# VectorE gating, a 64x64 triangular inverse and a loop set inside the sum, in a hybrid attention, RWKV-7 and expert block

## The chip, the cores and the metric

The kernel runs on one core of one Trainium2 chip. The metric is device time in microseconds (us) of one execution of the whole block. The engines are TensorE (PE for matmuls, PEld for its weight loads), VectorE (DVE), ScalarE (ACT), GpSimd (POOL) and SyncE (SP, which issues DMAs here).

## What is computed

One decoder layer over 256 tokens of width 2048: eight heads of attention beside sixteen heads of RWKV-7 time mixing, an output projection, then a mixture of 128 x 128 single-neuron experts, of which each token takes 16 in each of 8 heads. What matters of the reference:

```python
def rwkv7_time_mix(...):                       # 16 heads of 64
    def step(state, inp):
        rt, wt, kt, vt, at, bt = inp
        sa = jnp.einsum('bhij,bhj->bhi', state, at)
        state = (state * wt[:, :, None, :] + sa[..., None] * bt[:, :, None, :]
                 + vt[..., :, None] * kt[..., None, :])
        y = jnp.einsum('bhij,bhj->bhi', state, rt)
        return state, y

def peer_ffn(x, wq, sub_keys, u, v):
    q = (xt @ wq).reshape(T, H, 2, PEER_HALF)
    s = jnp.einsum('thpc,hpnc->thpn', q, sub_keys).astype(jnp.float32)
    sv, si = lax.top_k(s, K)
    cand = (sv[:, :, 0, :, None] + sv[:, :, 1, None, :]).reshape(T, H, K * K)
    best, bi = lax.top_k(cand, K)
...
    expert = (i1 * PEER_NKEYS + i2).astype(jnp.int32)
    gates = jax.nn.softmax(best, axis=-1)
    def chunk(args):
        xc, ec, gc = args
        hpre = jnp.einsum('cd,chkd->chk', xc, u[ec]).astype(jnp.float32)
        act = (jax.nn.gelu(hpre, approximate=False) * gc).astype(x.dtype)
        return jnp.einsum('chk,chkd->cd', act, v[ec])

def reference(...):
        h = h + jnp.concatenate([attn, rw], axis=-1) @ w_out[l]
        h = h + peer_ffn(rmsnorm(h, norm2_g[l]), peer_wq[l], peer_sub_keys[l], peer_u[l], peer_v[l])
    return rmsnorm(h, final_g)
```

## The kernel before, in words

All matmuls are made nearly float32 by splitting an operand into a high and a low part, each multiplied in one pass. For weights, `prefetch` loads a half of a weight block ("raw", 512 KB, SP), ScalarE rounds it to the high part (`whi`, L204) and VectorE subtracts to get the low part (`wlo`, L205). Three slots hold split halves, so that about two halves are ready ahead of PE. The list `halves` gives the order in which all weights are loaded and split. The order of the instructions on each engine is set by a scheduler at build time: generators `yield` numbers that say how much time a piece of work is meant to take, and the scheduler puts pieces side by side by those; nothing is reordered at run time, and each engine works strictly in its order.

The stages, by what PE does. *Projections* (7 to 540 us): `products()` runs the loras, then eight head pairs of RWKV (three blocks of weights each, L218 to L220), then eight attention heads; after each piece, `step_all` moves up to four live chains (`rwkv`, `attn`) on by a step. An `rwkv` chain treats two heads of 64 at once, as a block diagonal 128x128 matrix in each of four chunks. It has to invert a unit triangular matrix, and does so in five doublings (L484 to L505): VectorE transposes X (L493), PE multiplies M by it (L496, `pw`), VectorE masks the product into `wm` (L498), PE multiplies that by XT (L502, `px`), VectorE adds to XT (L504). That is 5 doublings x 8 pairs = 40 groups on each of the two matmul lines. *Output* and *queries* follow (540 to 736), with scores and choices of experts prepared.

*Hidden stage* (736 to 1568): for each of the 128 keys (a key is 128 experts), 16 matmuls on L240 and 16 on L242 give the experts' first products; the low parts' sum is `part` (L1137 on ScalarE, L1138 on VectorE), and ScalarE applies gelu (L1122) into `A`, eight keys to a tile. Beside this run, paced by the list `beside`, the choices of experts (`both_choices`), the tables of gates (`tables`, written to memory as `gate_d`), `places`, which gives every expert a row in a list sorted by which of the two token tiles chose it, and `scatter`: as soon as places are known, near 1219, for each key the gates (`gt`, loaded by GpSimd for eight keys at a time from `gate_d`, L1075) are multiplied on `A` (L1093, on GpSimd but for the last two keys), and GpSimd sends the gated rows to their places with an indirect DMA (L1107).

*Sum* (1573 to 2029): the sorted rows are read back in blocks of 128 experts (L1200, SP), each block's second weights are gathered by an indirect DMA (L1205, GpSimd), both are split (L248 ScalarE, L249 VectorE), and PE adds the products into eight accumulators, four for each token tile (L1192 to L1194, 12 matmuls a tile and block). There are C0 = 28 blocks for tile 0 alone, C1 = 28 for tile 1 alone and MID = 52 for both, 24 matmuls each. Experts chosen by both tiles beyond 52 blocks would be summed by a run-time loop (L1264) whose count is read from `nblk`; it stands behind all unrolled blocks, and its body closes the accumulators. Behind it VectorE adds the accumulators to the residual (`yr`, L1295), and the last norm and the stores follow.

Of the kernel before, what the change touches and what calls it, by code (L numbers as in the profile page):

```python
# [10 lines left out]
F32 = mybir.dt.float32  # L11
F32R = mybir.dt.float32r
BF16 = mybir.dt.bfloat16
I32 = mybir.dt.int32
# [48 lines left out]
C0, C1, MID, DN = 28, 28, 52, 2  # L63
# [5 lines left out]
def consts():  # L69
# [6 lines left out]
    c[:, K_MSK:K_MSK + P] = same & (p[:, None] < p[None])  # L76
# [3 lines left out]
    for i in range(6):  # L80
        n = 1 << i
        lv = (p[:, None] // (2 * n) == p[None] // (2 * n)) & (p[:, None] % (2 * n) >= n) & (p[None] % (2 * n) < n)
        c[:, K_LV + i * P:K_LV + (i + 1) * P] = lv
        if i == 0:
            c[:, K_M1T:K_M1T + P] = lv.T
# [69 lines left out]
def block_kernel(ctx: ExitStack, tc: tile.TileContext, x, cols, consts, w_lora, w_gate, w_rkv, w_qkv,  # L155
# [25 lines left out]
    for w, n in ((w_gate, 2), (w_rkv, 3 * RJ), (w_qkv, 3 * AH)):  # L181
        halves += [(w[m, i].rearrange("p k c -> p (k c)"), HK * P) for m in range(n) for i in range(2)]
# [163 lines left out]
    wms = [p1.tile([P, NC, P], F32, name=f"wm{i}") for i in range(1, 6)]  # L346
# [8 lines left out]
    mska = kc(K_MSK, 128).rearrange("p (h t) -> p h t", h=2).unsqueeze(1).to_broadcast([P, 2, 2, CH])  # L355
    mskr = kc(K_MSK + 128, 192).unsqueeze(1).to_broadcast([P, 2, 192])
# [3 lines left out]
    idb = ident.unsqueeze(1).to_broadcast([P, NC, 128])  # L360
# [15 lines left out]
    def rwkv(j, r, k, vv):  # L376
# [82 lines left out]
        for q in range(0, NC, 2):  # L459
            pc = bank("pc", [P, 4, 128])  # L460
            for c in range(2):
                for i, src in enumerate((nbd, kbd)):
# [3 lines left out]
            nc.vector.tensor_tensor(M[:, q:q + 2, 0:128].rearrange("p a (h t) -> p a h t", h=2),  # L466
                                    pc2[:, :, 0:CH].unsqueeze(2).to_broadcast([P, 2, 2, CH]), mska, op=ALU.mult)
            nc.vector.tensor_tensor(M[:, q:q + 2, 128:320], pc2[:, :, CH:], mskr, op=ALU.mult)
            yield

        XT = W("XT", [P, NC, 128], 2)
        lv = lambda i: kc(K_LV + i * 128, 128)
        nc.vector.tensor_tensor(XT, M[:, :, 0:128], kc(K_M1T, 128).unsqueeze(1).to_broadcast([P, NC, 128]),
# [10 lines left out]
        for i in range(1, 6):  # L484
            n = 1 << i
            nblk = P // (2 * n)
# [13 lines left out]
            px = bank("px", [P, NC, CH])  # L500
            for c in range(NC):
                nc.tensor.matmul(o4(px)[:, c], wm[:, c, :], hi_(XT)[:, c], start=(c == 0), stop=(c == NC - 1),  # L502
                                 skip_group_check=True)
            nc.vector.tensor_tensor(hi_(XT), hi_(XT), o4(px), op=ALU.add)  # L504
            yield  # L505

        y = tmp("y", "y")[:, :S]
        Z = None
        for c in range(NC):
# [15 lines left out]
            nc.tensor.matmul(sa_p, XT[:, c, :], r0, start=True, stop=True)  # L525
# [113 lines left out]
    def products():  # L639
# [18 lines left out]
        for j in range(RJ):  # L658
            while len(live) > 4:
                step_all()  # L660
# [12 lines left out]
        state["pools"] = [spl]  # L673
        for h in range(AH):
            while len(live) > 4:
                step_all()
# [8 lines left out]
            clear(1)  # L685

# [236 lines left out]
    def table(t):  # L923


        while t not in chosen:
            yield 0
# [77 lines left out]
    def places():  # L1005
# [39 lines left out]
        for t, n, base in ((0, C0, 0), (1, C1, B1)):  # L1045
# [5 lines left out]
            yield 1.5  # L1051
# [28 lines left out]
    def gated(i2, eng=nc.gpsimd):  # L1080

        if i2 % 7 == 0:
            rows[0] = big("at")
            n = min(7, NKEY - i2)
            eng.tensor_copy(rows[0][:, 0:n * ROW].rearrange("p (n c) -> p n c", c=ROW)[:, :, T].bitcast(I32),
                                  eint[:, i2:i2 + n])
# [6 lines left out]
        eng.tensor_tensor(at[:, 0:T].rearrange("p (q t) -> p q t", q=KT),  # L1093
# [4 lines left out]
    def scatter():  # L1098
# [4 lines left out]
        for i2 in range(NKEY - DN):  # L1103
# [11 lines left out]
            yield 1.5  # L1115
# [38 lines left out]
    beside = [[both_choices(), 0.55, 0.0], [tables(), 0.38, 0.0], [scatter(), 1.0, 0.0]]  # L1154
# [168 lines left out]
```

## Time and profile before

| | us |
|---|---|
| median of 3 runs | 2051.95 (2043.92 to 2052.5) |
| profiled execution | 2048.21 |
| its span, first to last instruction | 2046.3 |
| PE busy | 1935.7 (95%) |
| VectorE busy | 1437.7 (70%) |
| ScalarE busy | 1062.9 (52%) |
| GpSimd busy | 712.1 (35%) |

The span is what the trace covers; the 1.9 us between it and the execution's time lie around it. Busy time of PE counts overlapping records from the first start to the last modelled end, so that 95% does not mean that PE does 95% of what it could: how far apart the same matmuls start tells more. The mean granted clock was 0.981 of full speed. The rows below are from this one execution; times in them are us from the span's start.

### The profile page before, as it was taken

Reading aid. Unit: us, or ns where it says so; the run is one execution under the profiler, and the core shown is the slowest. Engines: PE = TensorE matmul, PEld = TensorE weight load, DVE = VectorE, ACT = ScalarE, POOL = GpSimd, SP = SyncE. Lnnn points to the kernel's source line nnn. Section 1 sums busy time; section 2 is a strip of 40 time slices with the busy share of each in tenths; the row PEclk is TensorE's granted clock in tenths of the full one; section 3 lists DMA queues with packets and bytes.
Section 4 is the critical chain, followed back from the end, with each engine's and each line's share of the span. In section 5 each row is a group of like instructions: output and inputs, shape, how many; then the busy total and the mean of one; then the engine's idle time right before and its main releaser. Section 6 shows DMA issues by size and latency. Waiting matters only on the chain. (4 is left out here: it accounts for less than half of the span.)

```text
span 2046.3 us, 31447 instructions
## 1 busy us (share of the span) xinstructions
PE 1935.7 (95%) x11804; PEld 1723.3 (84%) x11804; DVE 1437.7 (70%) x2090; ACT 1062.9 (52%) x1696; POOL 712.1 (35%) x654
## 2 busy tenths in 40 slices
PE   7888999999999999999999999887998999999996
PEld 6788999999879998878888888776887788888885
DVE  6766878766556888999878866544755666666665
ACT  4534554345455444677676744433444555555554
POOL 7211211100000000023424269998986333333322
PEclk9999999999999999999999999998999999999998
DMA  8999322225576666556666678786888887878783
GB/s 248 258 247 246 98 87 87 88 83 146 190 227 198 184 180 188 173 175 197 215 195 217 196 237 264 248 267 229 270 267 271 343 284 280 296 286 293 281 297 141
DMA packets 135291, 443.91 MB, mean 217 GB/s; under 512 B 14369, under 2 KB 52257, under 8 KB 118497
## 3 DMA queue, kind: packets, MB, share of 16 engines
q1 hardware_dynamic: 106992, 289.24, 47.7%
q0 software_dynamic: 28144, 152.65, 20.4%
q8 instruction: 93, 1.52, 0.3%
q14 instruction: 62, 0.50, 0.1%
HBM read 380.07 MB, written 61.76 MB: 216 GB/s over the span
## 5 line engine op out<-in xcount | busy, mean ns | idle before, releaser
L205 DVE TENSOR_TENSOR wlo<-raw,whi 128x1024 fp32r<-128x1024 f32 (+1 forms) x408 | 569.6, 1402 | 301.1 <-ACT whi L204 291.9
L240 PE MATMUL ps_gm<-nx,whi 128*128 128x512 f32 x2048 | 731.8, 400 | 24.9 <-ACT whi L204 21.9
L204 ACT ACTIVATE whi<-raw 128x1024 fp32r<-128x1024 f32 (+1 forms) x408 | 429.5, 1055 | 384.2 <-issue 89.5
L242 PE MATMUL ps_gm<-nx,wlo 128*128 128x256 f32 x2048 | 579.4, 283 | 14.2 <-DVE wlo L205 14.2
L240 PEld LDWEIGHTS ps_gm<-nx,whi 128*128 128x128 f32 x2048 | 387.8, 189 | 112.6 <-ACT whi L204 22.6
L242 PEld LDWEIGHTS ps_gm<-nx,wlo 128*128 128x128 f32 x2048 | 390.3, 191 | 20.1 <-DVE wlo L205 19.7
L249 DVE TENSOR_TENSOR vlo<-vraw,vhi 128x2048 fp32r<-128x2048 f32 x108 | 247.9, 2297 | 151.6 <-ACT vhi L248 146.1
L248 ACT ACTIVATE vhi<-vraw 128x2048 fp32r<-128x2048 f32 x108 | 205.9, 1913 | 156.3 <-DVE vlo L249 146.8
L1205 POOL DMA_INDIRECT vraw<-in_v_dram,ag x108 | 145.1, 1343 | 294.8 <-PE ps_gm L1194 210.0
L218 PE MATMUL ps_gm<-xh,whi 128*128 128x256 f32 x640 | 192.7, 301 | 0.8 <-ACT whi L204 0.8
L220 PE MATMUL ps_gm<-xh,wlo 128*128 128x256 f32 x640 | 185.1, 289 | 3.2 <-DVE wlo L205 3.1
L219 PE MATMUL ps_gm<-xl,whi 128*128 128x256 f32 x640 | 185.6, 290 | 0.0
L1107 POOL DMA_INDIRECT rows_d<-at,place x126 | 169.5, 1345 | 36.9 <-POOL at L1093 15.8
L951 POOL TENSOR_TENSOR mt<-gc 128x1024 f32<-128x1024 f32 x16 | 39.7, 2482 | 345.5 <-ACT gc L979 345.5
L1122 ACT ACTIVATE A<-part 128x256 f32<-128x256 f32 x128 | 53.1, 415 | 166.7 <-DVE part L1138 131.3
L1093 POOL TENSOR_TENSOR at<-A,gt 128x256 f32<-128x256 f32 x126 | 129.2, 1041 | 5.4 <-DMA gt<-gate_d 3.6
L220 PEld LDWEIGHTS ps_gm<-xh,wlo 128*128 128x128 f32 x640 | 122.8, 192 | 4.6 <-DVE wlo L205 4.2
L218 PEld LDWEIGHTS ps_gm<-xh,whi 128*128 128x128 f32 x640 | 122.9, 192 | 1.9 <-ACT whi L204 1.2
L219 PEld LDWEIGHTS ps_gm<-xl,whi 128*128 128x128 f32 x640 | 122.9, 192 | 0.7
L807 POOL DMA_DIRECT2D skb<-in_sk_dram x16 | 8.6, 540 | 250.7 <-ACT mh L248 167.7
L945 ACT ACTIVATE ob<-ob,pick 128x128 f32<-128x128 f32 x256 | 83.9, 390 | 19.6 <-DVE ob L937 19.6
L373 POOL TENSOR_TENSOR df<-ext 128x256 f32<-128x256 f32 (+1 forms) x28 | 23.8, 850 | 155.3 <-DVE ext L371 142.4
(1521 smaller groups left out, 3925.5 us busy)
## 6 DMA issues: line engine op xcount, KB each, us to landing
raw<-in_u_dram SPq DMA_DIRECT2D x256, 512.0 KB, 4.1
raw<-in_w_rkv_dram SPq DMA_DIRECT2D x48, 512.0 KB, 7.3
raw<-in_w_qkv_dram SPq DMA_DIRECT2D x48, 512.0 KB, 3.6
rows_d<-zt SPq DMA_DIRECT2D x23, 1028.0 KB, 15.8
raw<-in_w_out_dram SPq DMA_DIRECT2D x32, 512.0 KB, 3.9
raw<-in_wq_dram SPq DMA_DIRECT2D x32, 512.0 KB, 3.6
gate_d<-gc SPq DMA_DIRECT2D x16, 1024.0 KB, 6.5
gt<-gate_d POOLq DMA_DIRECT2D x16, 1024.0 KB, 9.0
```

The costliest lines, as they stand in the source:

```text
L204: nc.scalar.activation(hi[:, :n], raw[:, :n], AF.Copy)
L205: state["dve"] = nc.vector.tensor_tensor(lo[:, :n], raw[:, :n], hi[:, :n].bitcast(F32), op=ALU.subtract)
L218: nc.tensor.matmul(ps, a, xh(kt), start=first and k == 0, stop=False)
L219: nc.tensor.matmul(ps, a, xl(kt), start=False, stop=False)
L220: state["mm"] = nc.tensor.matmul(ps, b, xh(kt), start=False, stop=last and k == HK - 1)
L240: nc.tensor.matmul(ps.rearrange("p z t -> p (z t)"), hi[:, k * P:(k + 1) * P], x_.rearrange("p z t -> p (z t)"), start=i + k == 0, stop=Fa ...
L242: state["mm"] = nc.tensor.matmul(ps[:, 0, :], lo[:, k * P:(k + 1) * P], x_[:, 0, :], start=False, stop=i == 1 and k == HK - 1, skip_group_ ...
L248: nc.scalar.activation(hi, src, AF.Copy)
L249: nc.vector.tensor_tensor(lo, src, hi.bitcast(F32), op=ALU.subtract)
L1093: eng.tensor_tensor(at[:, 0:T].rearrange("p (q t) -> p q t", q=KT), As[i2 // 8][:, k, :].rearrange("p (q t) -> p q t", q=KT), g.rearrange( ...
L1107: s_ = nc.gpsimd.indirect_dma_start(out=rows_d, out_offset=bass.IndirectOffsetOnAxis(ap=place[:, i2:i2 + 1], axis=0), in_=at, in_offset=None)
L1205: nc.gpsimd.indirect_dma_start(out=raw, out_offset=None, in_=vf, in_offset=bass.IndirectOffsetOnAxis(ap=ag[:, T:ROW].bitcast(I32), axis=0))
```

## The change

The diff, cut to its core:

```diff
-C0, C1, MID, DN = 28, 28, 52, 2
+C0, C1, MID, DN = 28, 28, 51, 2
...
+    ORDER = [("r", 0), ("r", 1)] + [x for j in range(2, RJ) for x in (("r", j), ("a", j - 2))] + [("a", AH - 2), ("a", AH - 1)]
...
-    wms = [p1.tile([P, NC, P], F32, name=f"wm{i}") for i in range(1, 6)]
+    wms = [p1.tile([P, NC, CH], F32, name=f"wm{i}") for i in range(1, 6)]
...
+    both = [slice(0, 64), slice(64, 128)]
...
-        XT = W("XT", [P, NC, 128], 2)
+        XT = W("XT", [P, NC, CH], 2)
...
-            X = W("X", [P, NC, 128], XB)
+            X = W("X", [P, NC, CH], XB)
             nc.vector.transpose(X.rearrange("p c s -> p (c s)"), XT.rearrange("p c s -> p (c s)"))
-            pw = bank("pw", [P, NC, CH])
+
+            pw = bank("pw", [P, NC, CH // 2])
             for c in range(NC):
-                nc.tensor.matmul(o4(pw)[:, c], M[:, c, 0:128], lo_(X)[:, c], start=(c == 0), stop=(c == NC - 1),
-                                 skip_group_check=True)
+                for hs in both:
+                    nc.tensor.matmul(o4(pw)[hs, c], M[hs, c, 64:128], lo_(X)[hs, c], start=True, stop=True,
+                                     skip_group_check=True)
...
+        XB_ = W("XB", [P, NC, 128], 2)
+        bd(XB_, XT)
...
+        for k, (what, n) in enumerate(ORDER):
+            while len(live) > 4:
+                step_all()
+            if what == "a":
+                state["pools"] = [spl]
+            yield from (pair if what == "r" else head)(n)
...
-        while t not in chosen:
+        while 0 not in chosen or 1 not in chosen:
...
-            yield 1.5
+            yield 2.6
...
-    def gated(i2, eng=nc.gpsimd):
+    def gated(i2):
...
-        eng.tensor_tensor(at[:, 0:T].rearrange("p (q t) -> p q t", q=KT),
+        nc.vector.tensor_tensor(at[:, 0:T].rearrange("p (q t) -> p q t", q=KT),
...
-            yield 1.5
+            yield 2.0
...
-    beside = [[both_choices(), 0.55, 0.0], [tables(), 0.38, 0.0], [scatter(), 1.0, 0.0]]
+    beside = [[both_choices(), 0.6, 0.0], [tables(), 0.45, 0.0], [scatter(), 1.0, 0.0]]
...
+        if k == 40:
+
+            count = nc.values_load(nblk[0:1, 0:1], min_val=0, max_val=128,
+                                   skip_runtime_bounds_check_because="a count of at most 16384 experts in blocks of 128")
+            with tc.For_i(MID, count, 1) as i:
+                rows[2] = rows[1]
+                ag, _ = rows_at(i * P + BM)
+                rows[1] = rows[2]
+                block((0, 1), *divided(ag, gather(ag)), False)
```

Four things, then. VectorE makes all multiplies by the gates and the small copies of row numbers beside them; GpSimd keeps the loads of `gt` and the scatters, and the numbers that pace `scatter`, `places`, `both_choices` and `tables` are others (the tables of both tiles start when both choices are done). The triangular inverse keeps each head's 64x64 matrix by itself: the two heads of a pair lie on partitions 0 to 63 and 64 to 127, masks, X, XT and `wm` are 64 columns wide instead of 128, each doubling has eight matmuls of 64x64 weights by 32 columns where it had four of 128x128 by 64, and one block diagonal (`XB`) is made at the end, by GpSimd, for the steps that follow. The projections' blocks come interleaved, RWKV pairs 0, 1, 2, attention head 0, pair 3, head 1 and so on, and the list of halves with them. And 51 blocks for both tiles are unrolled instead of 52, with the run-time loop set inside the unrolled sequence; the last unrolled block of each tile closes its accumulators.

Line numbers of the changed kernel are a little higher: L1093 becomes L1106, L1107 L1120, L1075 L1088, L205 L211, L1138 L1151, L496 L502, L502 L509, L1264 L1278.

GpSimd, from the first gates on, before: each multiply of `A` by `gt` stands ahead of the scatter (`rows_d`) of its row, and the loads of the next `gt` between them.

```order
L1075 DMA gt_13032<-gate_d 128x16x128
L1085 COPY at<-eint 128x7
L1075 DMA gt_13060<-gate_d 128x16x128
L1093 TENSOR_TENSOR at<-A_8199,gt_13032 128x256 x7
L1107 DMA rows_d<-at,place 39936x257 x7
L1085 COPY at<-eint 128x7
L1093 TENSOR_TENSOR at<-A_8199,gt_13032 128x256
L1093 TENSOR_TENSOR at<-A_8687,gt_13060 128x256
L1107 DMA rows_d<-at,place 39936x257 x2
L1075 DMA gt_13178<-gate_d 128x16x128
L1093 TENSOR_TENSOR at<-A_8687,gt_13060 128x256 x2
```

The same place on GpSimd after:

```order
L1088 DMA gt_13443<-gate_d 128x16x128
L1088 DMA gt_13476<-gate_d 128x16x128
L1120 DMA rows_d<-at,place 39936x257 x9
L1088 DMA gt_13624<-gate_d 128x16x128
L1120 DMA rows_d<-at,place 39936x257 x8
L1088 DMA gt_13783<-gate_d 128x16x128
L1120 DMA rows_d<-at,place 39936x257 x4
L1088 DMA gt_13937<-gate_d 128x16x128
L1120 DMA rows_d<-at,place 39936x257 x12
```

The multiplies are gone from GpSimd; a load of `gt` stands behind 4 to 14 scatters. They are now on VectorE, after `place` is written (L1073), among the low parts of the weights (L211) and the sums `part` (L1151), of which there is one a key:

```order
L1073 CAST place<-wk 128x128
L1098 COPY at<-eint 128x7
L211 TENSOR_TENSOR wlo<-raw,whi 128x1024
L1151 TENSOR_TENSOR part<-part,ps_gm 128x256
L1106 TENSOR_TENSOR at<-A_8539,gt_13443 128x256 x5
L211 TENSOR_TENSOR wlo<-raw,whi 128x1024
L1106 TENSOR_TENSOR at<-A_8539,gt_13443 128x256 x3
L1106 TENSOR_TENSOR at<-A_9039,gt_13476 128x256
L211 TENSOR_TENSOR wlo<-raw,whi 128x1024
L1151 TENSOR_TENSOR part<-part,ps_gm 128x256
L1106 TENSOR_TENSOR at<-A_9039,gt_13476 128x256 x5
```

Before, VectorE had only L205 and L1138 there. Between this `part` and the next two stand nine multiplies and then seven; further on come keys with none.

PE at the loop, after: the loop's count and branch stand behind the products of the first 36 blocks, and matmuls of the unrolled blocks follow behind the loop's body.

```order
L1207 MATMUL ps_gm<-vhi,al__17545 128x512
L1276 TENSOR_LOAD nblk
L1278 COMPARE_AND_BRANCH
L1278 UNCONDITIONAL_BRANCH x2
L1334 BRANCH_PREFETCH_HINT
L1205 MATMUL ps_mm<-vhi,ah 128x512
```

Before, the same rows stood behind the products of the last block:

```order
L1194 MATMUL ps_gm<-vhi,al__19260 128x512
L1262 TENSOR_LOAD nblk
L1264 COMPARE_AND_BRANCH
L1264 UNCONDITIONAL_BRANCH x2
L1318 BRANCH_PREFETCH_HINT
L1192 MATMUL ps_mm<-vhi,ah 128x512
```

The loop moved forward past 71 blocks on PE, and on the other engines past the blocks that they had prepared.

## Rows read from the trace of the kernel before

**Rows 1.** Table of windows, by stage; x is the number of instructions
```profile
core 0: us, PE busy (x) PEld busy (x) DVE busy (x) ACT busy (x) POOL busy (x), PEclk, DMA share, GB/s
0.00:200.00 200.00, 164.67 (x1251) 157.84 (x1252) 134.59 (x220) 86.95 (x137) 68.42 (x107) 0.97 1.01 252
200.00:540.00 340.00, 335.06 (x2695) 325.22 (x2694) 249.42 (x494) 159.40 (x301) 37.26 (x46) 1.00 0.35 104
840.00:960.00 120.00, 111.79 (x680) 98.20 (x679) 119.38 (x182) 81.79 (x169) 29.21 (x18) 1.00 0.58 181
1219.00:1568.00 349.00, 318.11 (x1774) 274.55 (x1773) 201.68 (x167) 148.75 (x222) 310.95 (x276) 0.96 0.79 256
1568.00:1592.00 24.00, 14.70 (x51) 11.09 (x49) 8.47 (x10) 9.24 (x13) 6.90 (x7) 0.80 0.96 341
1600.00:2000.00 400.00, 400.00 (x1766) 331.22 (x1765) 257.92 (x197) 219.38 (x196) 131.09 (x98) 1.00 0.81 290
...
1375.00:1400.00 25.00, 7.82 (x29) 6.38 (x30) 4.92 (x5) 5.27 (x8) 22.41 (x25) 0.59 0.48 155
```

**Rows 2.** The table of windows for line L240 alone (PE, PEld, PEclk, DMA)
```profile
740.00:840.00 100.00, 100.00 (x289) 53.87 (x289) 1.00 0.65 189
1219.00:1568.00 349.00, 314.68 (x887) 168.55 (x886) 0.96 0.79 256
```

**Rows 3.** Waits of ScalarE, 1219 to 1568: total us, times, longest us
```profile
ACT A L1122 <- POOL at L1093: 30.7, 2, 21.8
```

**Rows 4.** Groups of VectorE (busy us, mean ns), 740:840, then 1219:1568
```profile
L205 DVE TENSOR_TENSOR wlo<-raw,whi 128x1024 fp32r<-128x1024 f32 x36 | 43.7, 1215 | 11.4 <-ACT whi L204 11.3
...
L205 DVE TENSOR_TENSOR wlo<-raw,whi 128x1024 fp32r<-128x1024 f32 x110 | 182.7, 1675 | 146.8 <-ACT whi L204 138.9 <-PE ps_gm L240 6.0 <-PE ps_gm L242 1.4
L1138 DVE TENSOR_TENSOR part<-part,ps_gm 128x256 f32<-128x256 f32 x55 | 22.6, 410 | 0.0
```

**Rows 5.** Instructions of L1093: ns min/median/max, first and last start
```profile
L1093 POOL TENSOR_TENSOR at<-A,gt x126: 843/942/1997, 1205.2 to 1562.2; 128x256 f32<-128x256 f32 x126
L1093 DVE TENSOR_TENSOR at<-A,gt x2: 621/662/704, 1567.1 to 1572.9; 128x256 f32<-128x256 f32 x2
```

**Rows 6.** The page's groups: the scatter (busy us, mean ns, idle before)
```profile
L1107 POOL DMA_INDIRECT rows_d<-at,place x126 | 169.5, 1345 | 36.9 <-POOL at L1093 15.8
```

**Rows 7.** Line L1075, the loads of gt: from issue to landing
```profile
DMA to landing us min/median/max: 6.6/9.0/9.9
```

**Rows 8.** Instructions of line L496: ns min/median/max
```profile
L496 PEld LDWEIGHTS ps_pw<-X,M x320: 186/192/192, 96.7 to 431.3; 128*128 128x128 f32 x160
L496 PE MATMUL ps_pw<-X,M x320: 217/275/295, 96.8 to 431.4; 128*128 128x64 f32 x160
```

**Rows 9.** Timeline of PE (start, us): a group and the next matmul
```profile
246.70 1.00 PE L496 MATMUL ps_pw<-X,M 128*128 128x64 f32 x8
247.52 0.36 PE L218 MATMUL ps_gm<-xh,ml 128*128 128x256 f32 x1
```

**Rows 10.** Groups by form: a weight load of 96 columns
```profile
L220 PEld LDWEIGHTS ps_px<-xh,wlo 128*96 128x96 f32 x8 | 1.3, 162 | 0.0
```

**Rows 11.** Instructions of L493 (transpose) and L498 (multiply)
```profile
L493 DVE STREAM_TRANSPOSE X<-XT x40: 685/702/714, 95.6 to 429.8; 128x512 f32<-128x512 f32 x40
...
L498 DVE TENSOR_TENSOR wm<-ps_pw,kr x40: 356/425/427, 97.9 to 432.3; 128x256 f32<-128x256 f32 x40
```

**Rows 12.** The timeline at the end: last matmul, first and last addition
```profile
2028.80 0.39 PE L1194 MATMUL ps_gm<-vhi,al__19260 128*128 128x512 f32 x1
2029.58 0.69 DVE L1295 TENSOR_TENSOR yr<-yr,ps_mm 128x512 f32<-128x512 f32 x1 [7.86 <-PEq L1264]
...
2037.63 0.67 DVE L1295 TENSOR_TENSOR yr<-yr,ps_gm 128x512 f32<-128x512 f32 x1
```

**Rows 13.** The loop's line, PE's sequencer
```profile
L1264 PEldq EVENT_SEMAPHORE  x13: 51/51/51, 2029.2 to 2031.0; - x13
```

**Rows 14.** Line L1205, the gathers: from issue to landing
```profile
DMA to landing us min/median/max: 5.3/7.2/17.0
```

More of the change, by code (lines that the diff above doesn't have):

```diff
@@ L75, in consts @@
     same = p[:, None] // 64 == p[None] // 64
-    c[:, K_MSK:K_MSK + P] = same & (p[:, None] < p[None])
+    c[:, K_MSK + 64:K_MSK + P] = (p[:, None] % 64) < np.arange(64)[None]
     c[:, K_MSK + P:K_MSK + 192] = (p[:, None] % 64) <= np.arange(64)[None]
@@ L180, in block_kernel @@
         halves += [(w_lora[m, i].rearrange("p k c -> p (k c)"), HK * LOR) for m in range(2)]
-    for w, n in ((w_gate, 2), (w_rkv, 3 * RJ), (w_qkv, 3 * AH)):
-        halves += [(w[m, i].rearrange("p k c -> p (k c)"), HK * P) for m in range(n) for i in range(2)]
+    ORDER = [("r", 0), ("r", 1)] + [x for j in range(2, RJ) for x in (("r", j), ("a", j - 2))] + [("a", AH - 2), ("a", AH - 1)]
+    blocks_ = [(w_gate, m) for m in range(2)]
+    for what, n in ORDER:
+        blocks_ += [((w_rkv if what == "r" else w_qkv), 3 * n + i) for i in range(3)]
+    halves += [(w[m, i].rearrange("p k c -> p (k c)"), HK * P) for w, m in blocks_ for i in range(2)]
     KP = (4, 5, 6, 7, 0, 1, 2, 3)
@@ L490, in rwkv @@
             wm = wms[i - 1]
[L492 removed]
+            X = W("X", [P, NC, CH], XB)
             nc.vector.transpose(X.rearrange("p c s -> p (c s)"), XT.rearrange("p c s -> p (c s)"))
[L494 removed]
+            pw = bank("pw", [P, NC, CH // 2])
             for c in range(NC):
[L496 to L497 removed]
+                for hs in both:
+                    nc.tensor.matmul(o4(pw)[hs, c], M[hs, c, 64:128], lo_(X)[hs, c], start=True, stop=True,
+                                     skip_group_check=True)
             nc.vector.tensor_tensor(lo_(wm), o4(pw), lo_(lv(i).unsqueeze(1)).to_broadcast([P, NC, nblk, n]), op=ALU.mult)
             yield
[L500 removed]
+            px = bank("px", [P, NC, CH // 2])
             for c in range(NC):
[L502 to L503 removed]
+                for hs in both:
+                    nc.tensor.matmul(o4(px)[hs, c], wm[hs, c, :], hi_(XT)[hs, c], start=True, stop=True,
+                                     skip_group_check=True)
             nc.vector.tensor_tensor(hi_(XT), hi_(XT), o4(px), op=ALU.add)
             yield
+        XB_ = W("XB", [P, NC, 128], 2)
+        bd(XB_, XT)
         y = tmp("y", "y")[:, :S]
@@ L524, in rwkv @@
             sa_p = bank("ch", [P, 128])
-            nc.tensor.matmul(sa_p, XT[:, c, :], r0, start=True, stop=True)
+            nc.tensor.matmul(sa_p, XB_[:, c, :], r0, start=True, stop=True)
             sa = W("sa", [P, 128], 3)
@@ L657, in products, with pair @@
         state["pools"] = [spl, spl, spare[0]]
-        for j in range(RJ):
-            while len(live) > 4:
-                step_all()
+        def pair(j):
             got = []
@@ L672, in products, with head @@
             clear(2)
[L673 to L676, printed above, removed]
+        def head(h):
             got = []
@@ L1223, in block_kernel @@
         with tc.issue_after(state["gelu"].ins), tc.issue_after(u_end.ins):
-            ah, al_ = halves_of(gated(i2, nc.vector)[:, 0:T])
+            ah, al_ = halves_of(gated(i2)[:, 0:T])
         for i in range(2):
@@ L1260, in block_kernel @@
                 block((t,), *cut[j], ends[t] == j)
-    count = nc.values_load(nblk[0:1, 0:1], min_val=0, max_val=128,
-                           skip_runtime_bounds_check_because="a count of at most 16384 experts in blocks of 128")
-    with tc.For_i(MID, count, 1) as i:
-        ag, _ = rows_at(i * P + BM)
-        block((0, 1), *divided(ag, gather(ag)), True)
+        if k == 40:
[6 more added lines that the diff above has]
+                block((0, 1), *divided(ag, gather(ag)), False)
     gf = mp.tile([P, D], F32, tag="ml", name="gf")
```

25 lines of the change are left out of this document (12 added, 13 removed).

## The prediction

> **What bounds the kernel now.** First I read the table of windows [rows 1]: each engine's busy time by stretch, cut where the stages change. TensorE (PE) is busy 335.06 of 340 us in the projections and 400.00 of 400 in the sum. So PE bounds the kernel: a PE cycle taken away is worth its full time, and an edit on another engine only what PE loses there. PE loses time in five places: the first 200 us (164.67 busy, DMA share 1.01, so the loads bound it), 840 to 960 (111.79 of 120, VectorE 119.38 of 120), the stretch in which gated rows are scattered, 1219 to 1568, the change of stage at 1568, and the end.
>
> The busy share hides most of the third, so I count matmuls [rows 2]. From 740 to 840 there are 289 of line L240 in 100 us, 0.346 us each with their L242; a key has 16, so a key takes 5.54 us. From 1219 to 1568 there are 887 in 349 us, where 887 x 0.346 = 306.9 would do: **42 us are lost**, in 55 keys. The table of waits shows how [rows 3]: ScalarE waited twice for the multiply on GpSimd, 30.7 us in all, 21.8 in one go; there, from 1375 to 1400, PE was busy 7.82 of 25 us at a granted clock of 0.59 [rows 1]. And VectorE's half of a weight split, L205, took 1675 ns on the mean against 1215 early on, while GpSimd multiplied beside it [rows 4].
>
> **The change part by part**, against the profiled run's 2048.21 us.
>
> *VectorE gates all rows.* A multiply is 942 ns on GpSimd in the median and 662 on VectorE [rows 5]. The 126 are 126 x 0.66 = 83 us more on VectorE; if L205 gets its early duration back, 110 x (1.675 - 1.215) = 51 us less. On the mean that fits: a key's two L205, one L1138 and one gate are 2 x 1.215 + 0.41 + 0.66 = 3.5 us of 5.54. But the new order doesn't spread them: 21 gates stand in three keys, then none for four keys, then 28 in some four, 21 in three, 21 in three, 15 in two, and one a key after that. In a burst of 21 VectorE needs 3 x 2.84 + 21 x 0.66 = 22.4 us where PE wants 3 x 5.54 = 16.6; halves split in advance cover about 3 us (one half's 2.77), so PE waits about 3. By the same sum the five bursts come to 3 + 5 + 3 + 3 + 1 = 15 us. Second, VectorE works in order, and a gate needs its group's gates, which GpSimd loads between the scatters. The third load stands behind nine scatters, 9 x 1.35 = 12.1 us after the burst began [rows 6], and lands 9.0 us later [rows 7], at 21 us; VectorE comes to the first gate that needs it after 16 x 0.66 and two keys' other work, at 16. It stands 5 us, and behind it stand the L205 that PE needs. Gone through row by row with these durations, five gates wait (5.6, 6.2, 2.0, 4.7 and 5.5 us) and PE loses 41 us in all; with landings of 5 us it is 25, with 11 us 50. So the 42 us that go, ScalarE's wait for GpSimd, come back as VectorE's wait for loads: **0**, from -17 to +16 (9 by late landings, 7 for the clock: after the stop at 1568, PE was busy 14.70 us with 51 records at clock 0.80 [rows 1], where 51 x 0.227 = 11.6 would do; 3 us, two or three times).
>
> *Paces of choices, tables and places.* The tables now wait until both choices are done, so that VectorE's heavy part is spread. What can be won is the 8.2 us that PE is idle from 840 to 960 [rows 1]: **-6**, from -8 to +8, the far end if such a stretch comes once more.
>
> *Inverse on 64x64 tiles.* Before, there are 80 groups, 40 of L496 and 40 of L502, of 4 matmuls with 2 records each; L496 has 320 records [rows 8]. From the start of a group of 8 records to the next matmul it is 247.52 - 246.70 = 0.82 us [rows 9]; over all groups the starts are 0.112 apart, 640 x 0.112 = 72 us. After, a group has 8 matmuls with half the weight columns and half the moving columns: 1280 records. No row shows a 64-column weight load. If a record costs half, nothing changes; if it costs as much as now, +72; if the two of a pair, on partitions 0 to 63 and 64 to 127, run at once, -36. The nearest row is the 96-column load, 162 ns [rows 10] against 192 for 128 [rows 8]: it shrinks with its columns. I take 0.060 a record: **+5**. VectorE's transpose, its multiply and the addition after it, of half the width, save 40 x (0.35 + 0.21 + 0.21) = 31 us [rows 11] (the addition, not shown, taken as the multiply); GpSimd, busy 37.26 of 340 there [rows 1], makes eight block diagonals more. With PE at 335 of 340 this hardly counts. The interleaved heads give PE attention work earlier, while the last RWKV pair's chain now runs on into the output stage. Together **-3**, from -8 to +6 (the 4.9 idle us and some of the first stretch, against a few late steps of the last pair).
>
> The Trainium skill speaks against this part: "TensorEngine Tiling (Array Packing)", Key Properties, says that a change of the tiling mode, not just of the tile, drains the TensorE. No row here has such a change; rival 1 prices it from rows. The same list says that different tiles can load weights and multiply in parallel, by which the term would be the -36.
>
> *One block less, and the loop moved.* The routing, worked out from the reference's inputs, puts 6,438 experts into the blocks that both token tiles share, 50.3 blocks, so 51 hold them and the loop's body still never runs. One block of 24 matmuls goes, 400 / 1766 = 0.227 us each [rows 1]: **-5.4**. The loop's entry is a meeting of all engines, and at the end it holds the tail: PE's last matmul starts at 2028.80, VectorE's first addition, after 7.86 us idle, at 2029.58 [rows 12], and all eight additions, both norms and the stores follow until 2046.3. With the loop elsewhere, the last four blocks belong to token tile 1 alone, 4 x 12 x 0.227 = 10.9 us; beside them run tile 0's four additions and norm, less than the 8.1 us between the first and the last addition now. Left is tile 1's share: 2046.3 - 2037.63 = 8.7 from the last addition on, and some 0.4 to begin, 9.1 instead of 17.3: **-8.2**, from -10 to -4 (if both tiles' additions still queue on VectorE). In the middle the meeting costs PE its 13 event waits, 2029.2 to 2031.0 [rows 13], and a branch: **+2.5**. Behind it stand GpSimd's gather of block 41 and VectorE's splits. PE then has two blocks split and two more gathered, four of 1.48 tiles x 2.72 = 4.0 us, 16 us; the gather is issued in some 1.35 and lands in 7.2 us in the median, 17.0 at most [rows 14], which leaves 7 us for its split. Covered; at 17.0 PE would stand some 6.
>
> **Sum:** 0 - 6 + 5 - 3 - 5.4 - 8.2 + 2.5 = -15.1, so 2033.1 against the profiled run. That run lies 3.7 us under the median of the runs (2051.95) and over the lowest (2043.92); against the median it is 2036.9. I give **2034**.
>
> **Rivals.**
> 1. *Switching tiles costs more than the tiles save* (slower). There are 160 switches, one before and one after each group. A record of L496 lasts 275 ns [rows 8] where the next starts after 112; if the array must run empty at each, that is 160 x 0.163 = 26 us up to 160 x 0.275 = 44 us, and PE has no slack to hide it: 2059 to 2077. A price per record that doesn't shrink gives up to 2100. It decides from 0.16 us a switch. For it: PE is full there. Against: 80 groups among 2700 records of that stretch, and what is lost may be only the weight load made in advance. Chance 0.22.
> 2. *The gating stage gets worse by as much as the rest brings* (no change). Loads land late while scatters and weights share the DMA engines (share 0.79 [rows 1]) and PE's stops cost clock: +16, 2049. For: VectorE in order, with the splits behind each wait. Against: landings were 9.9 us at most [rows 7]. Chance 0.20.
> 3. *A smooth gating stage, or quadrants at once.* Freed of multiplies, GpSimd may load gates early enough that only the bursts' 15 of the 42 us stay: -27, 2006. Or the inverse's term is -36 in place of +5: 1992. Chance 0.07 and 0.06.
> 4. *The count needs a 52nd block*: the body runs once, read and gather (7.2 each, say) and matmuls in a row, about +20 in place of -5.4: 2058. The 50.3 speaks against it. Chance 0.02.
>
> **How the numbers follow.** The forecast has 0.43, with 2022 to 2044 as its own range by the bounds of the small terms. The range takes in rival 2, the near half of rivals 1 and 3: **2005 to 2066**. A measurement of this kernel can tell about 0.5%, 10 us. Faster by more: 0.39 of the forecast and 0.13 of rival 3, 0.52. Within: 0.04 of the forecast, 0.18 of rival 2 and 0.04 of rival 1, 0.26. Slower: 0.18 of rival 1, 0.02 of rival 2, 0.02, together 0.22.
>
> **What would show it.** Afterwards: L240 at about 0.39 us in the gating stage (0.346 were smooth), VectorE idle on the loads of gt before the gates, and no wait of ScalarE for GpSimd; the groups of the inverse followed by the next matmul 0.9 to 1.0 us after their start (over 1.1 is rival 1); tile 0's additions before PE's last matmul, and 9 us from there to the end; a gap of 2 to 3 us on PE some 36 blocks into the sum. I am wrong if the groups take over 1.1 us, or if PE loses under 25 or over 58 us in the gating stage.

## The result, and the profile after

The changed kernel takes 2073.55 us (median of 4 runs, 2071.49 to 2077.22) against 2047.93 of the kernel before on the same chip: a ratio of 1.0138 (95% interval 1.0109 to 1.0167), **slower by 1.4%**, where I had forecast 2034 and faster, and outside my range of 2005 to 2066. The profiled execution spans 2072.8 us against 2046.3, 26.5 more.

The difference splits at places that both traces have, by the starts of the same matmuls (first L240 / L246, the first of key 72, the last of key 127, the sum's, the end):

| stretch | predicted, us | measured, us |
|---|---|---|
| projections, output, queries (inverse, order) | +2 | -15.9 (735.9 to 719.9) |
| keys 0 to 71 (paces) | -6 | +2.4 |
| keys 72 to 127 (gates on VectorE) | 0 | **+55.4** (352.1 to 407.4) |
| change of stage, first blocks of the sum | 0 | -7.0 |
| the loop's meeting in the middle | +2.5 | +2.3 |
| one block less | -5.4 | -5.4 |
| tail behind the last matmul | -8.2 | -5.3 |
| sum | -15.1 | +26.5 |

The block's -5.4 is 24 matmuls at their spacing, and the change of stage is what the other rows leave. One stretch decides it. The table of windows after, columns as in [rows 1]:

```profile
0.00:200.00 200.00, 171.57 (x1481) 162.18 (x1482) 128.08 (x214) 85.71 (x137) 68.39 (x106) 0.95 0.99 256
200.00:540.00 340.00, 333.53 (x3180) 309.63 (x3178) 241.18 (x501) 175.91 (x322) 44.53 (x57) 0.99 0.35 112
840.00:960.00 120.00, 119.35 (x729) 105.81 (x728) 110.12 (x156) 81.34 (x167) 21.84 (x14) 1.00 0.60 193
960.00:1195.00 235.00, 222.00 (x1378) 197.47 (x1377) 187.56 (x199) 161.58 (x359) 98.08 (x66) 0.99 0.60 200
1219.00:1568.00 349.00, 270.23 (x1459) 231.84 (x1458) 193.68 (x269) 121.90 (x182) 202.78 (x133) 0.89 0.68 224
```

From 1219 to 1568 PE is busy 270.23 us where it was 318.11 [rows 1], at a granted clock of 0.89, and ScalarE and GpSimd do less as well: nobody is overloaded, all wait. A key costs 407.4 / 56 = 7.28 us, against 6.29 before and 5.54 without losses [rows 2]: PE loses 407.4 - 56 x 5.54 = 97 us. The waits of VectorE, then of PE, from 1202 to 1610 (total us, times, longest):

```profile
DVE at L1106 <- DMA gt<-gate_d: 75.2, 5, 18.6
```

```profile
PE ps_gm L246 <- DVE part L1151: 40.8, 7, 18.4
PE ps_gm L248 <- DVE wlo L211: 37.8, 7, 17.4
```

VectorE stood five times for the loads of gates, 75.2 us in all, and PE stood 40.8 + 37.8 = 78.6 us for what VectorE had not done. Part of the other 18 us is PE's clock behind these stops. PE started again at 1252.08 after 17.44 us of idling, at half the clock, and soon after was back at the full one (columns as above):

```profile
1252.00:1257.00 5.00, 4.92 (x16) 4.25 (x17) 2.72 (x4) 1.36 (x2) 4.38 (x4) 0.50 0.81 232
1260.00:1265.00 5.00, 5.00 (x30) 4.39 (x29) 1.22 (x1) 1.50 (x3) 1.59 (x2) 1.00 1.01 377
```

Before it was ScalarE that waited, 30.7 us [rows 3]. The first burst shows why one wait lasts 17 us; GpSimd's timeline, then VectorE's:

```profile
1217.52 7.60 POOL L1120 DMA_INDIRECT rows_d<-at,place  x1 [23.78 <-DVE at L1106]
1225.42 6.41 POOL L1120 DMA_INDIRECT rows_d<-at,place  x1 [0.30 <-DVE at L1106]
1232.13 0.97 POOL L1120 DMA_INDIRECT rows_d<-at,place  x1 [0.30 <-issue]
1233.41 0.97 POOL L1120 DMA_INDIRECT rows_d<-at,place  x1 [0.30 <-issue]
...
1239.78 0.97 POOL L1120 DMA_INDIRECT rows_d<-at,place  x1 [0.30 <-DMA rows_d<-at,place]
1240.74 1.21 POOL L1088 DMA_DIRECT2D gt<-gate_d  x1
```

```profile
1224.12 0.40 DVE L1151 TENSOR_TENSOR part<-part,ps_gm 128x256 f32<-128x256 f32 x1
1224.45 3.01 DVE L1106 TENSOR_TENSOR at<-A,gt 128x256 f32<-128x256 f32 x5
...
1229.73 1.21 DVE L211 TENSOR_TENSOR wlo<-raw,whi 128x1024 fp32r<-128x1024 f32 x1
1230.87 0.40 DVE L1151 TENSOR_TENSOR part<-part,ps_gm 128x256 f32<-128x256 f32 x1
1248.13 2.76 DVE L1106 TENSOR_TENSOR at<-A,gt 128x256 f32<-128x256 f32 x5 [16.86 <-DMA gt<-gate_d]
```

The first scatter is 7.60 us long and the second 6.41, where one takes 0.97 otherwise. VectorE goes from gate to split to gate without a pause until 1231.27, yet the first scatter is through at 1225.12 and the second at 1231.83: each about 1.0 us, the length of a free scatter, after a sum `part` began (L1151 at 1224.12 and 1230.87). That sum reads one operand from PSUM (`ps_gm`), where a gate (L1106) and a split (L211) read both from SBUF. So it goes throughout this trace. Of its thirteen scatters over 2.5 us eleven end 0.97 us (within 0.12) after the start of a `part` or of the copy of row numbers (L1098), which reads one tensor, and the other two 0.85 us after VectorE had stopped. Each of the nine `part` that began under such a scatter let it through; of nine copies, 0.15 us long, two did.

From 1231.83 on seven scatters go by at 1.27 us each. Only behind the ninth stands the load of the third group of gates, at 1240.74. It lands at about 1248.1, and VectorE, which had come to the gate that needs it at 1231.27, goes on there.

### The profile page after: what moved, and what is told of

It reads as the page before. It is cut to its first block, busy times and chain, and to the rows that moved or that the text cites. A ratio compares the mean times of both kernels' runs of the same rounds, so it can differ in the third digit from the quotient of the medians.

```text
span 2072.8 us, 32579 instructions
## 1 busy us (share of the span) xinstructions
PE 1925.9 (93%) x12420; PEld 1700.5 (82%) x12420; DVE 1437.8 (69%) x2216; ACT 1063.9 (51%) x1700; POOL 599.5 (29%) x517
## 5 line engine op out<-in xcount | busy, mean ns | idle before, releaser
L246 PE MATMUL ps_gm<-nx,whi 128*128 128x512 f32 x2048 | 737.4, 402 | 43.9 <-DVE part L1151 43.8
L211 DVE TENSOR_TENSOR wlo<-raw,whi 128x1024 fp32r<-128x1024 f32 (+1 forms) x418 | 527.0, 1263 | 254.8 <-ACT whi L210 254.3
L210 ACT ACTIVATE whi<-raw 128x1024 fp32r<-128x1024 f32 (+1 forms) x418 | 439.0, 1054 | 394.8 <-PE ps_gm L246 78.6
L246 PEld LDWEIGHTS ps_gm<-nx,whi 128*128 128x128 f32 x2048 | 391.0, 191 | 134.4 <-DVE part L1151 47.9
L1120 POOL DMA_INDIRECT rows_d<-at,place x126 | 194.2, 1541 | 199.1 <-DVE at L1106 169.3
L224 PE MATMUL ps_gm<-xh,whi 128*128 128x256 f32 x720 | 221.3, 307 | 2.5 <-ACT whi L210 2.5
L226 PE MATMUL ps_gm<-xh,wlo 128*128 128x256 f32 x720 | 207.1, 288 | 2.1 <-DVE wlo L211 2.1
L225 PE MATMUL ps_gm<-xl,whi 128*128 128x256 f32 x720 | 207.4, 288 | 0.0
L226 PEld LDWEIGHTS ps_gm<-xh,wlo 128*128 128x128 f32 x720 | 138.5, 193 | 3.9 <-DVE wlo L211 3.4
L225 PEld LDWEIGHTS ps_gm<-xl,whi 128*128 128x128 f32 x720 | 139.0, 193 | 0.8
L1106 DVE TENSOR_TENSOR at<-A,gt 128x256 f32<-128x256 f32 x128 | 79.3, 666 | 85.6 <-DMA gt<-gate_d 75.2
L950 DVE TENSOR_TENSOR ob<-iota,pick 128x512 f32<-128x512 f32 x64 | 72.6, 1135 | 3.2 <-POOL act L970 3.2
L224 PE MATMUL ps_gm<-yh,whi 128*128 128x256 f32 x256 | 73.6, 288 | 0.0
```

The source lines that it names most:

```text
L210: nc.scalar.activation(hi[:, :n], raw[:, :n], AF.Copy)
L211: state["dve"] = nc.vector.tensor_tensor(lo[:, :n], raw[:, :n], hi[:, :n].bitcast(F32), op=ALU.subtract)
L224: nc.tensor.matmul(ps, a, xh(kt), start=first and k == 0, stop=False)
L225: nc.tensor.matmul(ps, a, xl(kt), start=False, stop=False)
L226: state["mm"] = nc.tensor.matmul(ps, b, xh(kt), start=False, stop=last and k == HK - 1)
L246: nc.tensor.matmul(ps.rearrange("p z t -> p (z t)"), hi[:, k * P:(k + 1) * P], x_.rearrange("p z t -> p (z t)"), start=i + k == 0, stop=Fa ...
```

## The experiments

My theory after the result: **VectorE's gates keep GpSimd from writing scatters; the load of the next gates stands behind those scatters; VectorE, in order, waits for the load with PE's weight splits behind it.** Rivals: the load merely stands too late (nothing holds GpSimd up); VectorE has too much to do in the bursts; the new paces are to blame. The kernels below were timed beside the kernel before (2049.7 to 2052.0 in these sessions).

**Gates loaded on SyncE.** In the changed kernel:

```diff
-            nc.gpsimd.dma_start(gts[g], gate_d[:, :, g * P:(g + 1) * P])
+            nc.sync.dma_start(gts[g], gate_d[:, :, g * P:(g + 1) * P])
```

> The changed kernel with the loads of the gates issued by SyncE instead of GpSimd, so that they stand behind no scatter; VectorE still makes all multiplies, in bursts. My theory (GpSimd held up, loads queued behind scatters, VectorE waiting in order): VectorE's 75 us of waits for gates fall under 15, single scatters in a burst still take 5 to 7 us, PE loses only what the bursts cost, 15 to 30 us of the 97: about 2000 us (1995 to 2015). Rival A, the loads only stand too late in GpSimd's order and nothing holds GpSimd up: the same time, but scatters of about 1 us throughout. Rival B, VectorE has too much to do in the bursts: over 2045, with the waits gone and PE still waiting for L211.

2002.74 us, ratio to before 0.9773 (0.9748 to 0.9798): 71 us under the changed kernel, and under the kernel before too. VectorE's wait for gates falls from 75.2 to 3.9 us; PE is through with key 127 at 1539.8 instead of 1609.5. The wait of VectorE, the scatters and the keys' matmuls (ns min/median/max; first and last start):

```profile
DVE at L1106 <- DMA gt<-gate_d: 3.9, 3, 1.7
```

```profile
L1120 POOL DMA_INDIRECT rows_d<-at,place x126: 965/1168/8151, 1224.5 to 1533.1; - x126
```

```profile
L246 PE MATMUL ps_gm<-nx,whi x2048: 387/396/774, 725.4 to 1539.8; 128*128 128x512 f32 x187
```

The scatters are still up to 8.15 us long, now beside nobody who waits for them. So GpSimd is held up (the rival that nothing holds it up falls), and it matters only through the load queued behind. That VectorE has too much to do in the bursts falls as well: the bursts are the same, and keys 72 to 127 take 332.6 us instead of 407.4. Some 3 of the 71 us lie in the tail.

**Gates spread evenly.** In the changed kernel, loads on GpSimd again:

```diff
-            at = gated(i2)
+            with tc.issue_after(state["dve"].ins):
+                at = gated(i2)
```

VectorE's order then has two or three gates in most keys.

> The changed kernel with one addition: each gate's multiply is ordered behind the latest weight split that stood ahead of it in the program, so that VectorE has about three gates in every key instead of 21 in three keys and none in the next five. Engines, loads on GpSimd, counts and paces stay. My theory: without bursts GpSimd gets to write its scatters between VectorE's instructions, the loads of gates come in time, and PE loses 10 to 25 us in the stage instead of 97: about 1997 us (1985 to 2015), waits of VectorE for gates under 15 us. Rival: two-tensor instructions on VectorE hold GpSimd up as much when they are spread; then scatters sum to as much, the loads are late all the same: over 2040.

2007.63 us, ratio 0.979 (0.975 to 0.983), some 10 us over the middle of what I expected. There is no wait for gates left; the longest of what stands ahead of the gates, and the scatters:

```profile
  ACT A L1136: 8.1, 17
```

```profile
L1121 POOL DMA_INDIRECT rows_d<-at,place x126: 963/1100/5867, 1222.0 to 1533.0; - x126
```

The longest scatter is 5.87 us, at the six gates of the first key, and the mean falls from 1.54 to 1.23 us; key 127 ends at 1539.5, as with the loads on SyncE. The same instructions on the same engines cost 66 us less when they don't come in bursts.

**Both together.**

> Both: gates spread evenly on VectorE and the loads of gates on SyncE. My theory: with the bursts gone the loads' queue matters little, so it is within 8 us of the spread version alone, about 1992 us. Rival: the loads' place behind the scatters costs by itself, 15 us or more over this version.

2008.1 us (0.9799, 0.9763 to 0.9835): the same as spread alone, though 16 us over the 1992 that I had named. Either remedy takes away nearly the whole wait (3.9 us, none, and 2.5 with both are left), so the two don't add up. Why the queue is harmless with spread gates isn't separated: GpSimd gets its turns, but VectorE also comes to the third group of gates only in the fifth key instead of the third, and the scheduler set that group's load behind seven scatters instead of nine.

**One-tensor multiplies.** Which instructions hold GpSimd up? In the changed kernel:

```diff
-        nc.vector.tensor_tensor(at[:, 0:T].rearrange("p (q t) -> p q t", q=KT),
-                          As[i2 // 8][:, k, :].rearrange("p (q t) -> p q t", q=KT),
-                          g.rearrange("p q (t b) -> p q t b", b=8)[:, :, :, k], op=ALU.mult)
+        nc.vector.tensor_scalar(at[:, 0:T], As[i2 // 8][:, k, :], g[:, 0, k:k + 1], None, op0=ALU.mult)
```

> The changed kernel with each gate's multiply replaced on VectorE by one that takes a single tensor and one number per partition out of the same loaded gates (so the right gate per token is left out; the wait for the load stays). My theory in its narrow form (VectorE instructions that read two tensors from SBUF hold GpSimd up): scatters beside these multiplies take about 1 us, the loads come 5 to 12 us earlier, VectorE's waits for gates fall from 75 to about 25 us, the time to about 2025. Wide form (any VectorE work holds GpSimd up): scatters of 5 to 7 us remain, and the time stays within 10 us of 2073. Rival (GpSimd is not held up by VectorE at all): no change either, but then also scatters slow where VectorE is idle.

2036.5 us in one run. The multiply and the scatter beside it (ns min/median/max), and VectorE's wait:

```profile
L1106 DVE TENSOR_SCALAR at<-A,gt x128: 333/351/566, 1223.3 to 1573.5; 128x256 f32<-128x256 f32 x128
```

```profile
L1118 POOL DMA_INDIRECT rows_d<-at,place x126: 963/972/2393, 1223.9 to 1562.9; - x126
```

```profile
DVE at L1106 <- DMA gt<-gate_d: 52.6, 5, 13.4
```

No scatter is longer than 2.39 us, every one over 1.3 lay over an L211, which still reads two tensors, and the twelve that lay beside one-tensor multiplies alone took 1.12 at most. So the narrow form holds: it is instructions that read two tensors. But the waits fell to 52.6 only, not to 25, and the time to 2036.5, not 2025: a multiply takes 0.35 us here, so VectorE comes to the late load some 16 x 0.32 = 5 us earlier each time. Five times 5 us taken off, about 27 us are left. By that estimate some 48 of the changed kernel's 75 us are the hold-up and 27 the place and landing of the loads.

**Two one-tensor multiplies a gate**, to give VectorE back its time:

```diff
+        for src in (As[i2 // 8][:, k, :], at[:, 0:T]):
+            nc.vector.tensor_scalar(at[:, 0:T], src, g[:, 0, k:k + 1], None, op0=ALU.mult)
```

> As the run with one-tensor multiplies, but two of them for each gate, so that VectorE is busy as long per gate as in the changed kernel (2 x 0.35 us against 0.67) without any two-tensor multiply (again the right gate per token is left out; the scheduler sets the loads a little earlier among the scatters, behind 4 and 10 instead of 9 and 8). My theory: scatters in the bursts stay under 2.5 us, the waits for gates sum to 20 to 45 us instead of 75, time 2020 to 2045. Rival, VectorE's time in the bursts is what counts, not the form of the instruction: waits and time as in the changed kernel, 2065 or more.

2017.16 us in one run, 3 us under what I allowed, with waits far under the 20 to 45 us that I expected. VectorE's wait, and the scatters:

```profile
DVE at L1107 <- DMA gt<-gate_d: 3.1, 2, 2.1
```

```profile
L1119 POOL DMA_INDIRECT rows_d<-at,place x126: 967/1079/2056, 1223.4 to 1543.9; - x126
```

With VectorE as busy as in the changed kernel, no scatter passes 2.06 us and the wait is 3.1 us instead of 75.2. The rival (VectorE's time, not the form) falls. The 46 scatters over 1.3 us all lay over an L211. A part of this gain is the loads' earlier place, which the scheduler chose by itself; how much, this run can't tell.

**Multiplies back on GpSimd**, the changed kernel otherwise (`nc.vector` to `nc.gpsimd` in `gated`, but for the last two keys).

> The changed kernel with only the multiplies by the gates (and the small copies beside them) back on GpSimd; the paces, the inverse, the order and the loop stay changed. My theory: VectorE's bursts of gates keep GpSimd from writing its scatters, the load of the next gates stands behind nine scatters, and VectorE waits for it with the weight splits behind it; so the 55 us that the stretch from key 72 to key 127 lost against before go away: about 2018 us (2010 to 2030), no wait of VectorE for gates. Rival: the new paces (tables and places later, scatter slower) make the stretch slow whichever engine multiplies: 2045 or more.

2038.61 us (0.9937, 0.9913 to 0.996): between the two. The stretch itself came out as I expected, keys 72 to 127 in 343 us instead of 407. But with the new paces GpSimd, which multiplies and scatters, ends late. Its last scatter; ScalarE, which in its order waits for the rows to be read back, with a weight split behind; and PE's first matmuls that need the split and then the gathered weights:

```profile
1570.38 1.00 POOL L1120 DMA_INDIRECT rows_d<-at,place  x1 [0.28 <-POOL at L1106]
```

```profile
1577.05 0.42 ACT L254 ACTIVATE ah<-ag 128x256 fp32r<-128x256 f32 x1 [21.03 <-DMA ag<-rows_d]
1577.38 1.04 ACT L210 ACTIVATE whi<-raw 128x1024 fp32r<-128x1024 f32 x1
```

```profile
1578.47 0.80 PE L1205 MATMUL ps_ch<-whi,ah 128*128 128x512 f32 x1 [12.47 <-ACT whi L210]
...
1591.17 0.80 PE L1205 MATMUL ps_mm<-vhi,ah 128*128 128x512 f32 x1 [6.38 <-ACT vhi L254]
```

PE was through with the keys at 1548 and stood 12.47 and 6.38 us more at the change of stage. In the next run, with the old paces, the last scatter starts 3.9 us ahead of the last key's last L246; here it starts 22.2 behind it. So the miss of 20 us is the paces, which fit VectorE's gates and not GpSimd's; which of the numbers does it wasn't separated.

**The first part undone whole** (engine, paces, tables); inverse, order, 51 blocks and loop stay.

> The changed kernel with the whole first part undone (multiplies on GpSimd, paces and tables as before); inverse, interleaved order, 51 blocks and the loop inside the sum stay. From the two traces these three gave 15.9 us up to the first key and 5.4 + 5.3 - 2.3 = 8.4 us in the sum and the tail: about 2048 - 24 = 2024 us (2018 to 2030), with the gating stage as before (6.3 us a key). Rival: the gains ahead of the hidden stage depend on the paces, or a stage that starts earlier meets its loads later: 2035 or more.

2030.18 us (0.9894, 0.987 to 0.9918): 22 us under before, just past the far end of the expected span. Without its first part the change is a gain.

**Each other part alone**, in the kernel before:

> The kernel before with the 64x64 inverse alone. From the two traces a group and the matmul on each side of it take 0.585 + 0.208 + 0.223 = 1.016 us where they took 0.813 + 0.119 + 0.202 = 1.134, so 80 groups save 9.4 us: about 2048 - 9 = 2039 us (2034 to 2044). Rival: only the interleaved order brought the projections' gain, and what the groups save is lost by waiting: within 3 us of before.

2041.38 us, ratio 0.9954 (0.9939 to 0.997): 9.6 us under the 2051.02 of before.

> The kernel before with the interleaved order of RWKV pairs and attention heads alone. Projections and output ended 10 to 16 us earlier with inverse and order together; if the inverse is worth 9, the order is worth 1 to 7: about 2044 us (2040 to 2049). Rival: the order alone is worth the whole 10 to 16: 2035.

2049.8 us, 0.9993 (0.9975 to 1.0011): no difference, where I had expected 1 to 7 us.

> The kernel before with 51 blocks and the loop behind the 36th block alone. From the two traces: 5.4 us for the block, 5.3 for the tail, less 2.3 for the meeting of the engines: 8.4 us, about 2042 us against 2050 (2039 to 2045). Rival: the meeting in the middle delays the gathers and costs as much as the tail brings: 2046 or more.

2040.72 us, 0.9959 (0.994 to 0.9978): 8.9 us under the 2049.66 of before; the traces had added up to 8.4.

## Why the prediction was wrong

**The term that failed is the gating stage**, put at 0 with bounds of -17 and +16; it came out at +55.4. The kind of wait was the one I described; its size was wrong: 24 us of waits predicted and 75.2 measured, 41 us lost by PE predicted and 97 measured, past the 58 that I had named as a sign of being wrong. The failing step is "behind nine scatters, 9 x 1.35 = 12.1 us after the burst began [rows 6]": in the first burst the load was issued 1240.74 - 1217.52 = 23.2 us after the first scatter began. The step fails twice. The 1.35 is the length of a scatter; from one to the next it is 0.30 more (the timeline of GpSimd above). That makes each of the five waits some 9 x 0.30 = 2.7 us longer, by estimate 38 us instead of 24 and a loss of about 55 instead of 41, still far from 97. And the 1.35 was taken from a kernel in which VectorE didn't multiply gates: the two held scatters of the first burst alone add 7.60 + 6.41 - 2 x 0.97 = 12.1 us. [rows 4] showed that the engines hinder each other, L205 at 1675 ns beside GpSimd's multiply; I used it for VectorE's relief (rightly: L211 is at 1228 ns there now) and never asked what VectorE's 83 us of new two-tensor work does to GpSimd. The trace of before had the answer. Its scatters (line L1107: ns min/median/max), and two of them on GpSimd's timeline with VectorE's beside them:

```profile
L1107 POOL DMA_INDIRECT rows_d<-at,place x126: 961/1054/2045, 1219.8 to 1563.4; - x126
```

```profile
1219.83 2.04 POOL L1107 DMA_INDIRECT rows_d<-at,place  x1 [5.86 <-DVE place L1060]
1222.18 1.01 POOL L1107 DMA_INDIRECT rows_d<-at,place  x1 [0.30 <-issue]
```

```profile
1219.69 1.22 DVE L205 TENSOR_TENSOR wlo<-raw,whi 128x1024 fp32r<-128x1024 f32 x1 [0.76 <-ACT whi L204]
1222.47 1.23 DVE L205 TENSOR_TENSOR wlo<-raw,whi 128x1024 fp32r<-128x1024 f32 x1 [1.55 <-ACT whi L204]
```

The first began behind an L205 that ran to 1220.91 and took 2.04 us, 1.08 of them under it; the second began ahead of the next L205 and took 1.01. In all, 57 of the 126 took over 1.3 us there, every one of them over an L205, and none over 2.05.

The Trainium skill has a page on this that I should have weighed, "SBUF — State Buffer", Who interferes with whom: VectorE and GpSimd share a pair of ports, and a VectorE instruction with two SBUF inputs contends with a GpSimd instruction that reads SBUF. The runs agree: the scatter, whose row numbers stand in SBUF (`place`), is held up to 8.15 us; beside one-tensor multiplies alone it takes 1.12 at most. The same section infers that two-tensor instructions don't stall the writing of DMA descriptors. For plain loads the traces agree: the issue of a load of gt took 1.16 to 1.24 us in both kernels, three times wholly under an L205 in the kernel before. For these indirect scatters they don't.

**Inverse: within its bounds, with the wrong sign.** I took +5, between -36 and +72; counted on PE it is -9.4. The timeline of PE after, to set beside [rows 9], and the records:

```profile
246.39 0.39 PE L522 MATMUL ps_ch<-M,B 128*128 128x128 f32 x2
246.71 0.66 PE L502 MATMUL ps_pw<-X,M 64*64 64x32 f32 x16
247.29 0.38 PE L224 MATMUL ps_gm<-xh,whi 128*128 128x256 f32 x1
247.51 0.28 PE L225 MATMUL ps_gm<-xl,whi 128*128 128x256 f32 x1
```

```profile
L502 PE MATMUL ps_pw<-X,M x640: 212/220/241, 96.9 to 491.0; 64*64 64x32 f32 x160
```

A group goes from its start to the next matmul in 247.29 - 246.71 = 0.58 us instead of 0.82, with twice the records: pairs start 7 ns apart in the median, so the two halves do run at once. Rival 1 was real too, but small: the matmul ahead of a group holds 0.208 us instead of 0.119 before the group starts, the one behind it 0.223 instead of 0.202, so that a group with its neighbours takes 1.016 us instead of 1.134. Times 80 that is -9.4; the run of the inverse alone gives 9.6 less in its median, 6 to 13 by its interval. How well these agree is in part luck: in that run's trace (7.4 us less in its span) the first key comes only 4.3 us earlier, keys 72 to 127 take 7.8 less, and the change of stage 4.6 more. The switch in and out costs some 0.11 us a group, not 2 x 0.16. Both sentences that I cited from the Trainium skill ("TensorEngine Tiling (Array Packing)", Key Properties) fit what is seen: the smaller tiles, two at once, save 0.23 us a group, and entering and leaving them takes back half of it.

**Order of the heads:** -3 predicted with the inverse's side effects, none measured alone. Together with the inverse the first key came 9.8 to 15.9 us earlier in the traces, with the inverse alone 4.3, with the order alone 0.7 later. That the two help each other by a few us is possible, but kernels with the same inverse and order reached it anywhere from 719.9 to 726.1, and the run of the loop alone, the same as before up to there, at 738.8 instead of 735.9. So it stays open.

**Paces:** -6 predicted, +2.4 measured. The 8.2 us of idle PE from 840 to 960 did go (119.35 of 120), but 13 came back from 960 to 1195, 222.00 of 235, where before there were none. The stretch before, and PE's longest waits there after:

```profile
960.00:1195.00 235.00, 235.00 (x1472) 209.63 (x1471) 188.78 (x192) 167.55 (x360) 87.86 (x58) 1.00 0.66 208
```

```profile
PE ps_pw L982 <- ACT gc L992: 5.6, 2, 3.3
PE ps_gm L246 <- DVE part L1151: 2.8, 4, 1.2
PE ps_pc L1046 <- DVE tot L1040: 2.7, 1, 2.7
```

The tables' work (L982, L992) had moved there, and PE waits among it. The 2.7 us for `tot` aren't new: before, that wait of 3.5 us stood just behind 1195. My bounds had room for such a stretch, the forecast had not.

**Loop and block** were right, **the tail** came out short within its bounds. The gap on PE in the middle of the sum, and the last addition:

```profile
1780.86 0.39 PE L1207 MATMUL ps_gm<-vhi,al__17545 128*128 128x512 f32 x1
1783.24 0.50 PE L1205 MATMUL ps_mm<-vhi,ah 128*128 128x512 f32 x1 [1.99 <-issue]
```

```profile
2062.18 0.67 DVE L1311 TENSOR_TENSOR yr<-yr,ps_gm 128x512 f32<-128x512 f32 x1
```

2.38 us lie between two starts instead of 0.23: 2.2, and 2.3 with the two starts behind (I had 2.5). The loop's body didn't run: PE has 24 records less in the sum, one block's. The tail behind PE's last matmul (2060.59) is 12.2 us instead of 17.5 (2046.3 - 2028.80; my sum had 17.3): 5.3 gained, not 8.2. Of the missing 3 us 1.2 lie ahead of the last addition, which comes 1.6 us behind the last matmul instead of 0.4, with a multiply by the norm's weights (L1306) on VectorE in between. Most of the rest lies at the very end: GpSimd signals its end 2.7 us after SyncE has seen the stores through, where it was 1.1 before. In the two runs with the gates' loads on SyncE it is 0.3, and their tails are 9.2 and 9.5 us; what holds GpSimd there wasn't tried.

The change of stage, put at 0, brought 7.0 us: the last scatter starts 6.5 us ahead of the last key's last L246 (1603.0 and 1609.5), before 4.3 us (1563.4 and 1567.7), so the sum's first rows are there sooner. The twelve traces of this case bear that out. From the last L246 to the first matmul on gathered weights it is 16.8 to 17.8 us where the last scatter leads by 6.4 to 7.1, 22.1 where it leads by 3.9 or 4.3, 26.7 and 27.3 where it comes 4 later, and 43.0 where it comes 22.2 later.

Of the rivals, 2 (the gating stage gets worse by what the rest brings) had the right place and the right kind of wait, at a third of its price, but not its reason. The loads landed as they had before [rows 7]; they were issued late:

```profile
DMA to landing us min/median/max: 6.5/9.2/11.9
```

## What to carry to other kernels

Moving the multiplies from GpSimd to VectorE slowed what GpSimd kept, since here VectorE's instructions that read two tensors from SBUF held up the scatters. Ask what each engine holds up on the other, in both directions, and look for it in the trace of before as a duration with a wide spread (961 to 2045 ns). A load that an in-order engine will wait for should not be queued behind work that this very engine holds up; another queue or an even spacing cost one or two lines here and turned +1.4% into -2.3% or -2.1%. And count from one start to the next, not the length of a record.

## What the runs showed of the hardware

- An indirect scatter on GpSimd takes 0.97 us alone and up to 8.15 us while VectorE runs instructions with two tensors in SBUF back to back. It got its turn when VectorE paused or came to an instruction with one operand in SBUF at most: all sums with an operand in PSUM that began under a scatter of over 2.5 us (nine in the changed kernel, eleven with the loads on SyncE) let it through, and it ended about 0.97 us after they began. Beside one-tensor multiplies of about the same total time it stayed at or under 2.06 us, and those 2 us lay over an L211.
- Pairs of 64x64 matmuls on the two halves of the partitions start 7 ns apart, and a group of 16 records takes 0.58 us, against 0.82 for 8 records of 128x128; entering and leaving the smaller tiles costs about 0.11 us in all.
- A meeting of all engines in the middle of a stream of matmuls, with two blocks ready ahead, cost PE 2.2 us and nothing behind it.
